# Dot products of the modulation on VectorE in both attention stages

## The chip, the cores and the metric

One core of a Trainium2 chip runs the whole program. The metric is the device time of one execution in microseconds; the time given is the median of three. The core has five engines that each work through their own queue in order: TensorE (PE; its weight loads are PEld), VectorE (DVE), ScalarE (ACT), GpSimd (POOL) and SyncE (SP), which here only issues transfers.

## The reference

The reference is three mixer layers over 512 tokens of width 2048, two of a first kind and one of a second. The first two also carry 256 context tokens. Each layer begins with a modulation: a vector `c` is passed through silu and multiplied with a matrix of 2048 x 6144, which gives a shift, a scale and a gate for every feature.

```python
sh_l, sc_l, g_l = jnp.split(jax.nn.silu(c) @ w_mod[l] + b_mod[l], 3, axis=-1)
sh_c, sc_c, g_c = jnp.split(jax.nn.silu(c_ctx) @ w_mod[l] + b_mod[l], 3, axis=-1)
hl = xl * (1.0 + sc_l[:, None, :]) + sh_l[:, None, :]
parts_l = jnp.split(hl @ w_in[l], SPLIT_POINTS, axis=-1)
```

The modulated tokens are multiplied with `w_in`; the parts feed a short convolution, a differential attention with eight heads, and a pooling branch. Their outputs are joined, multiplied with `w_out`, gated, added to the input and normalised. The third layer has its own modulation (`w_ada_2`) from `c_2`, a banded attention and a wider convolution.

## The kernel before, in words

All products with `w_in` and `w_out` are done on TensorE in a split of each fp32 number into a high part and the rest. A weight tile arrives in `wraw` (L155), ScalarE rounds it to `whi` (L156), GpSimd or VectorE subtracts to get `wlo` (L140), and TensorE multiplies high with high, high with rest and rest with high (`mm3`, L160 to L163). In the attention stages `wlo` is always GpSimd's (`lo_plan`). A `unit` (L195) is one such product of 128 features: 16 steps, into one or two of four PSUM buffers `ps_m`.

An attention stage (`attention`, L450) goes through eight heads. Each head has four units (query, key, value, gate). Their evictions follow: `evict_q` and `evict_k` turn the results by position (L314 to L317, on VectorE and GpSimd) and split them (L326 to L340), and `evict_v` copies the values out of PSUM on ScalarE (L345, L346) and transposes them. The tiles `qr` and `vT` of these three share one buffer, and each of the two key tiles has one buffer. So the value's copy waits until the key's split is done, and the key's split until the scores of the head before have been read out of the old key.

`attend` (L361) then works on blocks of 128 queries. For each of the two maps of a head: scores on TensorE (L379), a row maximum (L384) and its negative (L386) on VectorE, the exponential with its sum on ScalarE (L393), a reciprocal on VectorE (L395). L398, L400 and L401 on VectorE join both maps, TensorE transposes (L408), ScalarE and VectorE split (L412, L413), and TensorE multiplies with the values (L418). L422 to L446 are the norm of the head's output. The scores have one buffer (`ps_s`).

The modulation's products are spread as side work. Rows of the transposed matrix have 2048 numbers; a dot product of one such row per partition with silu(c) is done in four quarters of 512 (`dots`, L779). For every quarter the vector is loaded and passed through silu (L788 to L793), then each block of 128 rows is loaded as `gw` (L801; two buffers in the attention stages) and multiplied with one vector or two. The sum over the 512 goes to one column of the result; after each quarter but the first the columns are added (L815).

There are two ways of doing one such product. With `pool_every` at 0 it is one operation on VectorE, which multiplies and sums (L809). With `pool_every` at 1 it is a product on GpSimd into a junk tile with one buffer (L805), and a copy on ScalarE that sums it (L806). The two attention stages had 1; the stages between and after them have 0.

`along` hands such a generator to the main work, and `advance` takes a few steps of it (3 or 4) after every unit, with a priority that is 800 places later than the main work's. The order of every engine's queue is made when the program is built: a planner goes through all instructions by priority and by its own estimate of when each can start. So a change to some instructions can move others. What is left of the side work is issued by `finish` at the end of the stage.

The first stage has 192 such products (32 for the pooling's gates, 128 and 32 for the modulations of the first and the second layer), each load of `gw` being used for two vectors. The second has 128, each load for one.

Of the kernel before, what the change touches and what calls it, by code (L numbers as in the profile page):

```python
# [46 lines left out]
def mixer_stack_kernel(ctx: ExitStack, tc: tile.TileContext, a: dict, out: bass.AP):  # L47
# [8 lines left out]
    def pool(name, side):  # L56
        return tc.tile_pool(name=name, bufs=1, side=side, reuse_waits="tile")
# [113 lines left out]
    def along(steps, n):  # L171
        side["steps"], side["n"] = steps, n
# [6 lines left out]
    def finish():  # L179
        advance(10 ** 4)  # L180
        side["n"] = 0
# [268 lines left out]
    def attention(ap_, aq, l, w, H, Hc, started=None):  # L450
        cx = Hc if l == 0 else None
        T = NT if l == 0 else NL
        for h in range(8):
            if h == 0 and started:
                uq, uk, uv, ug = started
            else:
                uq = unit(w, 16 + h, H, cx)
            Q = evict_q(ap_, aq, uq, T)
            if not (h == 0 and started):
                uk = unit(w, 24 + h, H, Hc)  # L460
            K = evict_k(ap_, aq, uk)
            if not (h == 0 and started):
                uv = unit(w, 32 + h, H, Hc)
            vT = aq.tile([128, NT], F32, name="vT", tag="qr", bufs=1)
            V = evict_v(ap_, uv, vT)
            if not (h == 0 and started):
                ug = unit(w, 40 + h, H, cx)
            SG = ap_.tile([128, T], F32, name="SG", tag="SG", bufs=1)
            for ps, o, n in ((ug.lat, 0, NL), (ug.cx, NL, NCX)):
                if ps is not None:  # L470
                    th = aq.tile([128, NL], F32, name="rsh", tag="rsh", bufs=1)
                    silu2(SG[:, o:o + n], ps, th[:, :n])
            attend(ap_, l, h, Q, K, V, SG, T)
        for e in EARLY:
            if e[0] == l:
                u = unit(w, 48 + e[1], H, cx)
                t = aq.tile([128, NT], F32, name="pu", tag="qr", bufs=1)
                nc.scalar.copy(t[:, :NL], u.lat)
                if l == 0:
                    nc.scalar.copy(t[:, NL:], u.cx)  # L480
                nc.sync.dma_start(PUd[e][:, :T], t[:, :T])
# [209 lines left out]
    pgb = const.tile([128, 2, 4], F32, name="pgb")  # L691
# [87 lines left out]
    def dots(xp, vecs, scale, srcs, dst, bufs, pool_every=0):  # L779

        n = len(srcs)
        for q in range(4):
            sl = slice(q * 512, (q + 1) * 512)
            vs = []
            for v, src in enumerate(vecs):
                t = xp.tile([128, 512], F32, name=f"gv{v}", tag=f"gv{v}", bufs=1)
                if isinstance(src, str):
                    nc.sync.dma_start(t, Gd[src][0, sl].partition_broadcast(128))  # L788
                else:
                    nc.sync.dma_start(t, a["cc"][src, sl].partition_broadcast(128))  # L790
                    th = xp.tile([128, 512], F32, name="gw", tag="gw", bufs=bufs)
                    nc.scalar.activation(th, t, AF.Tanh, scale=0.5)
                    nc.vector.scalar_tensor_tensor(t, th, 1.0, t, op0=ALU.add, op1=ALU.mult)  # L793
                vs.append(t)
            part = dst
            if q:
                t = const.tile([128, 2, 32], F32, name="gpart", tag="gpart", bufs=1)
                part = [t[:, v] for v in range(len(vs))]
            for i, src in enumerate(srcs):
                w = xp.tile([128, 512], F32, name="gw", tag="gw", bufs=bufs)  # L800
                nc.sync.dma_start(w, src[:, sl])  # L801
                for v, t in enumerate(vs):
                    if pool_every and (i * len(vs) + v) % pool_every == 0:
                        pr = xp.tile([128, 512], F32, name="gpr", tag="gj", bufs=1)
                        nc.gpsimd.tensor_tensor(pr, w, t, op=ALU.mult)  # L805
                        nc.scalar.activation(pr, pr, AF.Copy, scale=scale, accum_out=part[v][:, i:i + 1])  # L806
                        continue
                    junk = xp.tile([128, 512], F32, name="gpr", tag="gj", bufs=1)
                    nc.vector.scalar_tensor_tensor(  # L809
                        junk, w, scale, t, op0=ALU.mult, op1=ALU.mult, accum_out=part[v][:, i:i + 1]  # L810
                    )
                yield
            if q:
                for d, p in zip(dst, part):
                    nc.vector.tensor_tensor(d[:, :n], d[:, :n], p[:, :n], op=ALU.add)  # L815

    def mod_dots(xp, names, vecs, w, bias, n0, n1, bufs=2, pool_every=0):
        dst = [mods[nm][:, n0:n1] for nm in names]
        yield from dots(xp, vecs, 0.5, [w[i] for i in range(n0, n1)], dst, bufs, pool_every)
        for d in dst:  # L820
            nc.vector.tensor_tensor(d, d, P(bias)[:, n0:n1], op=ALU.add)

    def mod_dots1(xp, l, n0, n1, bufs=2, pool_every=0):
        return mod_dots(xp, (f"l{l}", f"c{l}"), (0, 1), a["w_mod"][l], f"b_mod{l}", n0, n1, bufs, pool_every)

    def mod_dots2(xp, n0, n1, bufs=2, pool_every=0):
        return mod_dots(xp, ("s",), (2,), a["w_ada"][0], "b_ada", n0, n1, bufs, pool_every)

    with pool("attn0", R) as ap_:
        along(itertools.chain(  # L830
            dots(ap_, ("sh_l", "sh_c"), 1.0, [a["w_gateT"][g] for g in range(4)], [pgb[:, 0], pgb[:, 1]], 2, 1),
            mod_dots1(ap_, 0, 32, 48, 2, 1),
            mod_dots1(ap_, 1, 0, 4, 2, 1),
        ), 3)
        attention(ap_, ap_, 0, w0, H, Hc, started=us)
        finish()
# [62 lines left out]

    lo_plan["cycle"] = "P"  # L900
    with pool("attn1", L) as ap_:
        along(mod_dots2(ap_, 2, 34, 2, 1), 4)
        attention(ap_, aq, 1, a["w_in"][1], H, Hc)
        finish()
    es_q.close()
# [67 lines left out]
    with pool("attn2", R) as ap_:  # L973
# [25 lines left out]
        for j in range(2):  # L999
# [3 lines left out]
            for s in range(2):  # L1003
                g, r = 2 * j + s, 64 * s
# [5 lines left out]
        for j in range(2):  # L1010
# [7 lines left out]
            for s in range(2):  # L1018
                g = 2 * j + s
# [278 lines left out]
```

## Time and profile before

| | us |
|---|---|
| median of 3 runs | 3577.58 (3574.09 to 3579.79) |
| the profiled execution's own time | 3577.58 |
| its span, first to last instruction | 3575.8 |
| TensorE busy | 3301.2 |
| VectorE busy | 2324.2 |
| ScalarE busy | 1519.0 |
| GpSimd busy | 1958.8 |
| first attention stage, about | 245 to 1035 |
| second attention stage, about | 1630 to 2290 |

The profile names an engine, the line of the kernel and the tiles (output <- inputs) of every instruction. A busy time is a sum of instructions; an idle time stands before an instruction, with the releaser that ended it. The granted clock is TensorE's, as a share of full speed.

### The profile page before, as it was taken

How to read it: one execution, taken by the hardware profiler on the slowest of the kernel's cores; microseconds unless marked ns; L12 is line 12 of the kernel's file. 1: busy time of each engine (PE TensorE's matmuls, PEld its weight loads, DVE VectorE, ACT ScalarE, POOL GpSimd, SP SyncE). 2: the span in 40 equal slices, each digit the busy share in tenths (PEclk: the TensorE clock that was granted, in tenths of full speed). 3: DMA queues.
4: the chain of work that ended last, by engine and by line, in shares of the span. 5: the costliest groups of instructions: out<-in, count | busy, mean ns of one | idle time of the engine just before them, and what ended most of it. 6: DMA issues, size and time to landing. Idle time of an engine off the chain costs nothing.

```text
span 3575.8 us, 48562 instructions
## 1 busy us (share of the span) xinstructions
PE 3301.2 (92%) x16850; PEld 2791.3 (78%) x16850; DVE 2324.2 (65%) x3649; ACT 1519.0 (42%) x3181; POOL 1958.8 (55%) x1436
## 2 busy tenths in 40 slices
PE   8898998989998899999999999998989899999997
PEld 7787887878886787778888888877668777777765
DVE  6845555555468538774565555585577899996576
ACT  2255666655431222243665654322445333345333
POOL 2356776765234543256877764587776444444432
PEclk8899999989998999999999999999999999999999
DMA  8744333333246447664554542586765222223565
GB/s 311 288 133 115 99 111 99 103 104 89 70 143 185 135 131 221 191 223 140 159 154 143 162 126 85 184 309 227 231 221 195 80 93 84 84 77 109 183 222 187
DMA packets 274150, 554.72 MB, mean 155 GB/s; under 512 B 30992, under 2 KB 40048, under 8 KB 265712
## 3 DMA queue, kind: packets, MB, share of 16 engines
q1 hardware_dynamic: 271344, 539.04, 46.9%
q0 software_dynamic: 2560, 12.58, 1.8%
q8 instruction: 132, 2.16, 0.3%
q14 instruction: 114, 0.93, 0.1%
HBM read 510.69 MB, written 28.23 MB: 151 GB/s over the span
## 4 chain that ended last, share of the span: by engine, by line
PE 49%; DVE 18%; DMA 12%; issue 8%; POOL 7%; ACT 6%; SPq 0%; DVEq 0%; POOLq 0%; ACTq 0%
PE ps_m L163 35%; DVE acc L989 5%; DMA wraw<-in_w_out_dram 5%; POOL wlo L140 3%; POOL gpr L805 3%; DVE gpr L809 2%; PE ps_m L232 2%; PE ps_s L379 2%; ACT whi L156 2%; DVE wlo L140 2%; PE ps_v L418 2%; DMA gw<-in_w_ada_dram 1%; PE ps_s L233 1%; PE ps_m L609 1%; DMA gv<-in_cc_dram 1%
## 5 line engine op out<-in xcount | busy, mean ns | idle before, releaser
L163 PE MATMUL ps_m<-h,whi 128*128 128x512 f32 (+1 forms) x4736 | 1611.2, 398 | 47.3 <-ACT vT L345 32.5
L140 POOL TENSOR_TENSOR wlo<-wraw,whi 128x512 fp32r<-128x512 f32 x768 | 1113.3, 1467 | 947.6 <-ACT whi L156 886.0
L163 PEld LDWEIGHTS ps_m<-h,whi 128*128 128x128 f32 x4736 | 899.9, 192 | 233.7 <-ACT vT L345 34.1
L156 ACT CAST whi<-wraw 128x512 fp32r<-128x512 f32 x1040 | 608.1, 618 | 881.1 <-DMA wraw<-in_w_out_dram 268.0
L163 PE MATMUL ps_m<-h,wlo 128*128 128x512 f32 (+1 forms) x2368 | 940.0, 397 | 0.1
L805 POOL TENSOR_TENSOR gpr<-gw,gv 128x512 f32<-128x512 f32 x320 | 425.8, 1331 | 240.9 <-ACT gpr L806 173.1
L163 PE MATMUL ps_m<-hc,whi 128*128 128x256 f32 x2048 | 554.5, 283 | 0.0
L163 PEld LDWEIGHTS ps_m<-h,wlo 128*128 128x128 f32 x2368 | 455.1, 192 | 93.8 <-POOL wlo L140 0.8
L163 PEld LDWEIGHTS ps_m<-hc,whi 128*128 128x128 f32 x2048 | 381.0, 190 | 3.4
L140 DVE TENSOR_TENSOR wlo<-wraw,whi 128x512 fp32r<-128x512 f32 x272 | 246.7, 921 | 202.3 <-ACT whi L156 201.7
L806 ACT ACTIVATE gpr<-gpr 128x512 f32<-128x512 f32 x320 | 201.8, 631 | 233.6 <-POOL gpr L805 232.9
L163 PE MATMUL ps_m<-hc,wlo 128*128 128x256 f32 x1024 | 288.9, 282 | 0.0
L989 DVE SCALAR_TENSOR_TENSOR acc<-gu,pack,acc 128x511 f32<-128x511 f32 (+24 forms) x240 | 232.7, 981 | 5.4
L609 PE MATMUL ps_m<-wlo,y 128*128 128x512 f32 x512 | 208.1, 407 | 21.2 <-POOL wlo L140 13.6
L809 DVE SCALAR_TENSOR_TENSOR gpr<-gw,gv 128x512 f32<-128x512 f32 x232 | 220.7, 951 | 8.4 <-DMA gw<-in_w_ada_dram 2.0
L610 PE MATMUL ps_m<-whi,y 128*128 128x512 f32 x512 | 204.2, 400 | 3.2 <-DVE y L140 3.2
L384 DVE TENSOR_REDUCE mx<-ps_s 128x1 f32<-128x768 f32 (+1 forms) x160 | 135.0, 844 | 102.0 <-PE ps_s L379 101.2
L163 PEld LDWEIGHTS ps_m<-hc,wlo 128*128 128x128 f32 x1024 | 194.9, 190 | 1.0
L608 PE MATMUL ps_m<-whi,y 128*128 128x512 f32 x512 | 183.3, 400 | 1.7 <-ACT y L582 0.8
L413 DVE TENSOR_TENSOR aTl<-ps_t,aTh 128x384 fp32r<-128x384 f32 (+1 forms) x144 | 77.4, 538 | 156.2 <-ACT aTh L412 156.0
L609 PEld LDWEIGHTS ps_m<-wlo,y 128*128 128x128 f32 x512 | 98.0, 191 | 56.5 <-POOL wlo L140 22.1
L379 PE MATMUL ps_s<-K,Q 128*128 128x384 f32 x576 | 133.3, 347 | 9.5 <-ACT E L393 5.2
(353 smaller groups left out, 5284.4 us busy)
## 6 DMA issues: line engine op xcount, KB each, us to landing
wraw<-in_w_in_dram SPq DMA_DIRECT2D x640, 256.0 KB, 2.9
wraw<-in_w_out_dram SPq DMA_DIRECT2D x384, 256.0 KB, 3.5
wm<-in_w_mod_dram SPq DMA_DIRECT2D x48, 1024.0 KB, 6.9
gw<-in_w_mod_dram SPq DMA_DIRECT2D x192, 256.0 KB, 3.4
gw<-in_w_ada_dram SPq DMA_DIRECT2D x136, 256.0 KB, 3.2
wm<-in_w_ada_dram SPq DMA_DIRECT2D x14, 1024.0 KB, 6.5
K<-K POOLq DMA_DIRECT2D x32, 384.0 KB, 4.4
gv<-in_cc_dram SPq DMA_DIRECT2D x40, 256.0 KB, 3.6
```

The costliest lines, as they stand in the source:

```text
L140: eng.tensor_tensor(lo, src, hi.bitcast(F32), op=ALU.subtract)
L156: nc.scalar.copy(hi[:, sl], raw)
L163: nc.tensor.matmul(ps, w, mv[part], start=(first and p == 0), stop=(last and p == 2))
L379: nc.tensor.matmul(o, Qm[:, q0:q0 + 128], kp[:, c * ncol:(c + 1) * ncol], start=i == 0, stop=i == 1)
L384: nc.vector.reduce_max(mx, sv, axis=AX.XY)
L608: nc.tensor.matmul(ps, yh, hi[:, sl], start=(k == 0), stop=False)
L609: nc.tensor.matmul(ps, yh, lo[:, sl], start=False, stop=False)
L610: nc.tensor.matmul(ps, yl, hi[:, sl], start=False, stop=(k == KT - 1))
L805: nc.gpsimd.tensor_tensor(pr, w, t, op=ALU.mult)
L806: nc.scalar.activation(pr, pr, AF.Copy, scale=scale, accum_out=part[v][:, i:i + 1])
L809: nc.vector.scalar_tensor_tensor(junk, w, scale, t, op0=ALU.mult, op1=ALU.mult, accum_out=part[v][:, i:i + 1])
L989: nc.vector.scalar_tensor_tensor(A[:, s:], U[:, :NL - s], wj(i), A[:, s:], op0=ALU.mult, op1=ALU.add)
```

## The change

Five calls lose their last two arguments. `bufs` is 2 by default as well, so only `pool_every` changes, from 1 to 0. With 0, the branch with L805 and L806 is not taken, and every product of the two stages becomes L809. The transfers, the quarters and the additions of L815 stay the same in the source.

```diff
@@ -828,9 +828,9 @@
     with pool("attn0", R) as ap_:
         along(itertools.chain(
-            dots(ap_, ("sh_l", "sh_c"), 1.0, [a["w_gateT"][g] for g in range(4)], [pgb[:, 0], pgb[:, 1]], 2, 1),
-            mod_dots1(ap_, 0, 32, 48, 2, 1),
-            mod_dots1(ap_, 1, 0, 4, 2, 1),
+            dots(ap_, ("sh_l", "sh_c"), 1.0, [a["w_gateT"][g] for g in range(4)], [pgb[:, 0], pgb[:, 1]], 2),
+            mod_dots1(ap_, 0, 32, 48),
+            mod_dots1(ap_, 1, 0, 4),
         ), 3)
         attention(ap_, ap_, 0, w0, H, Hc, started=us)
         finish()
@@ -899,7 +899,7 @@
     with pool("attn1", L) as ap_:
-        along(mod_dots2(ap_, 2, 34, 2, 1), 4)
+        along(mod_dots2(ap_, 2, 34), 4)
         attention(ap_, aq, 1, a["w_in"][1], H, Hc)
         finish()
```

## Rows read from the trace of the kernel before

**Rows 1.** The page, part 1: busy us, share of the span, instructions.

```profile
PE 3301.2 (92%) x16850; PEld 2791.3 (78%) x16850; DVE 2324.2 (65%) x3649; ACT 1519.0 (42%) x3181; POOL 1958.8 (55%) x1436
```

**Rows 2.** Stretches: length, busy PE, PEld, DVE, ACT, POOL, granted clock, DMA share, GB/s.

```profile
245.00:890.00 645.00, 578.10 (x3361) 510.98 (x3361) 365.72 (x640) 389.46 (x911) 436.97 (x342) 0.94 0.36 104
890.00:1035.00 145.00, 138.45 (x812) 122.34 (x811) 62.57 (x132) 59.94 (x118) 37.78 (x30) 0.96 0.26 78
1630.00:2130.00 500.00, 487.22 (x2695) 424.89 (x2694) 286.99 (x447) 289.27 (x658) 381.15 (x300) 0.99 0.51 146
2130.00:2290.00 160.00, 160.00 (x832) 137.33 (x831) 73.54 (x130) 69.57 (x129) 62.04 (x51) 1.00 0.28 90
```

**Rows 3.** PE's waits, 245 to 1035: us in total, times, longest.

```profile
PE ps_m L163 <- ACT vT L345: 32.5, 5, 8.9
PE ps_t L408 <- DVE E L401: 12.0, 3, 5.8
```

**Rows 4.** PE's waits, 1630 to 2290.

```profile
PE ps_t L408 <- DVE E L401: 7.2, 3, 4.2
```

**Rows 5.** Timeline of PE: start us, us, instruction, idle before it and its releaser.

```profile
434.39 0.69 PE L408 MATMUL ps_t<-ident,E 128*128 128x128 f32 x2 [5.82 <-DVE E L401]
```

**Rows 6.** Timeline of VectorE in the same stall.

```profile
427.60 4.32 DVE L400 TENSOR_SCALAR E<-E,rd 128x256 f32<-128x256 f32 x1
```

**Rows 7.** Timeline of GpSimd in the same stall.

```profile
427.45 0.57 POOL L341 DMA_DIRECT2D K<-K  x1 [1.22 <-DVE K L140]
428.04 1.29 POOL L805 TENSOR_TENSOR gpr<-gw,gv 128x512 f32<-128x512 f32 x1
429.28 2.48 POOL L140 TENSOR_TENSOR wlo<-wraw,whi 128x512 fp32r<-128x512 f32 x2
```

**Rows 8.** Groups, 890 to 1035: busy us, mean ns, idle before.

```profile
L400 DVE TENSOR_SCALAR E<-E,rd 128x256 f32<-128x256 f32 x4 | 1.6, 404 | 0.1
```

**Rows 9.** Timeline of VectorE in the second stage.

```profile
1901.00 7.14 DVE L398 TENSOR_TENSOR rd<-rd,neglam 128x1 f32<-128x1 f32 x1
```

**Rows 10.** The stretch of that operation, columns as in rows 2.

```profile
1901.00:1908.20 7.20, 4.17 (x19) 3.08 (x17) 7.16 (x2) 2.73 (x7) 7.12 (x6) 1.00 0.99 237
```

**Rows 11.** Groups, 2130 to 2290, columns as in rows 8.

```profile
L398 DVE TENSOR_TENSOR rd<-rd,neglam 128x1 f32<-128x1 f32 x8 | 1.3, 159 | 0.2
```

**Rows 12.** The stretch after the stall of rows 5, columns as in rows 2.

```profile
430.60:440.60 10.00, 6.21 (x16) 4.92 (x17) 8.39 (x12) 5.61 (x14) 5.32 (x5) 0.50 0.47 119
```

**Rows 13.** Tile gpr alone: busy DVE, ACT, POOL in two stretches, clock, DMA.

```profile
245.00:890.00 645.00, 0.00 (x0) 138.62 (x384) 252.66 (x192) 0.94 0.36 104
1630.00:2130.00 500.00, 0.00 (x0) 92.40 (x256) 173.14 (x128) 0.99 0.51 146
```

**Rows 14.** ScalarE's waits, 245 to 1035, columns as in rows 3.

```profile
ACT gpr L806 <- POOL gpr L805: 132.9, 105, 4.0
```

**Rows 15.** The page, part 5: busy us, mean ns, idle before, releaser.

```profile
L809 DVE SCALAR_TENSOR_TENSOR gpr<-gw,gv 128x512 f32<-128x512 f32 x232 | 220.7, 951 | 8.4 <-DMA gw<-in_w_ada_dram 2.0
```

**Rows 16.** Line L809: duration ns minimum, median, maximum, first and last start.

```profile
L809 DVE SCALAR_TENSOR_TENSOR gpr<-gw,gv x232: 670/693/2194, 1038.2 to 1515.1; 128x512 f32<-128x512 f32 x116
L809 DVE DVE_READ_ACCUMULATOR gpr<-gw,gv x232: 74/81/88, 1039.8 to 1516.6; 128x1 f32 x116
```

**Rows 17.** Groups, 245 to 890, columns as in rows 8.

```profile
L400 DVE TENSOR_SCALAR E<-E,rd 128x256 f32<-128x256 f32 x12 | 17.7, 1472 | 0.4
L398 DVE TENSOR_TENSOR rd<-rd,neglam 128x1 f32<-128x1 f32 x40 | 16.9, 422 | 1.3
```

**Rows 18.** Groups, 1630 to 2130, columns as in rows 8.

```profile
L398 DVE TENSOR_TENSOR rd<-rd,neglam 128x1 f32<-128x1 f32 x24 | 21.7, 906 | 0.8
```

**Rows 19.** GpSimd's waits, 1630 to 2290, columns as in rows 3.

```profile
POOL gpr L805 <- DMA gw<-in_w_ada_dram: 25.7, 18, 3.3
```

**Rows 20.** SP's queue's waits, 245 to 890, columns as in rows 3.

```profile
SPq L801 <- POOL gpr L805: 226.1, 74, 7.8
```

## The prediction

> **What bounds the kernel now.** I read the busy times first, then the stretches, then the waits, then single timelines. TensorE is busy 92% of the span and is the engine to watch [rows 1]. The change touches only the two attention stages, at 245 to 1035 us and 1630 to 2290 us. I cut each where its last product on GpSimd ends, at 890 and at 2130 us. In the first stage TensorE is idle 645 - 578.1 = 66.9 us (10.4%) while the dot products run, at a granted clock of 0.94, and 6.6 of 145 us (4.5%) at 0.96 after them. In the second it is idle 12.8 of 500 us (2.6%) at 0.99 with them, and not at all at 1.00 after them [rows 2]. So the first stage has something to win, and the second very little.
>
> What TensorE waits for in the first stage is led by ScalarE's copy of V out of PSUM (L345, 32.5 us in 5 waits) and VectorE's last softmax step (L401, 12.0 us in 3) [rows 3]. In the second L401 gives 7.2 us in 3 [rows 4]. These fall where one head ends and the next is prepared. One is shown: TensorE stands 5.82 us until 434.39 for L401 [rows 5]. Behind that lies L400 on VectorE, which took 4.32 us from 427.60, although the same form takes 0.404 us after the dot products. From 427.45 to 431.76 GpSimd ran a DMA issue, a product (gpr) and two subtractions (wlo), almost without a gap, and L400 ended 0.16 us after the last of them [rows 6 to 8]. L398 in the second stage took 7.14 us from 1901.00, with GpSimd busy in six operations for 7.12 us of the same stretch, where 0.159 us is its mean after the dot products [rows 9 to 11]. A stall costs twice: in the 10 us from 430.6 the granted clock is 0.50, which is 1.2 of 2.4 GHz [rows 12].
>
> **The change part by part.** Removed from GpSimd: 320 products, 252.7 us in the first stage and 173.1 us in the second. Removed from ScalarE: 320 sums with their accumulator reads, 138.6 and 92.4 us [rows 13], and the time in which its queue stood for a product, 132.9 us in the first stage [rows 14]. On ScalarE those waits stood ahead of the exponentials, the K copies and the V copy. The junk tile that passed from GpSimd to ScalarE and back now stays on one engine, so two waits per dot product go and none is added to it.
>
> Added to VectorE: 320 operations of the form of L809. Its floor is 0.693 us (the median) and its mean 0.951 us, with 0.08 us for the accumulator read [rows 15, 16]. I take 0.951 + 0.08 = 1.03 us, because GpSimd still runs wlo beside it: 192 x 1.03 = 198 us and 128 x 1.03 = 132 us. Given back: L398 falls to its mean after the dots, (422 - 159) ns x 40 = 10.5 us and (906 - 159) ns x 24 = 17.9 us, and the narrow form of L400 gives (1472 - 404) ns x 12 = 12.8 us [rows 8, 11, 17, 18]. VectorE then has 365.7 - 23.3 + 198 = 540 of 645 us (84%) and 287.0 - 17.9 + 132 = 401 of 500 us (80%), from 57% each [rows 2]. It fits, so VectorE doesn't become the bound by its sum. It can by its order.
>
> Term 1, the first stage's stalls. If the dot products cost TensorE nothing, the stretch would look like the one after them: (10.4 - 4.5)% of 645 = 38 us, and 0.02 of clock over 645 us = 13 us, 51 us together. Below, the least is nothing at all, if the stalls come from the order of the evictions alone. I take two thirds, 34 us, since in the stall shown (4.32 - 0.40) of 5.82 us was the wait behind GpSimd.
>
> Term 2, the second stage: 12.8 us of idle and 0.01 of clock over 500 us, 18 us at most, nothing at least. Two thirds is 12 us.
>
> Term 3, what the new operations cost at the ends of heads. In the 10 us after the stall shown VectorE was busy 8.39 us, so 1.6 us were free [rows 12]. Spread evenly, 192 operations over 645 us put three into such a stretch. One fits, two delay the K subtraction that stands behind them, and with it ScalarE's V copy and TensorE: 2 x 1.03 = 2.1 us for each of seven ends (eight heads share 790 us, so 645 us hold six to seven), 14 us, and 4 us for the half clock behind longer stalls: 18 us. The bounds are 0 us (all fall where VectorE waits anyway) and 3 x 2.19 us (the longest L809) x 7 = 46 us. Between heads I cost them at nothing: TensorE has the next head's projections to do, and in that cover the softmax may come late. Without it 198 us would show.
>
> Term 4, the DMA. In the second stage GpSimd stood 25.7 us in 18 waits for the row of w_ada to land [rows 19]. That wait is now VectorE's, and behind it in the queue stand the row maxima, reciprocals and subtractions, which ScalarE's exponentials and TensorE's transposes wait for. TensorE's work hides most: 4 us, a sixth, between 0 and 25.7. No DMA is added or moved in the source. SP's queue stood 226.1 us in the first stage for products to release the two gw buffers, with the weight loads behind it [rows 20]; VectorE releases them now, after one operation rather than after a product that itself waited for ScalarE. I count nothing for it.
>
> Sum: -34 - 12 + 18 + 4 = -24 us. The profiled execution took 3577.58 us for a span of 3575.8 us, and it is itself the median of the three runs, so no other correction: 3577.6 - 24 = 3553.6 us, forecast 3554.
>
> That GpSimd holds VectorE off is first of all the row of 7.14 us. The Trainium skill's page "SBUF — State Buffer" (Who interferes with whom) states why: a VectorE operation with two SBUF inputs shares a read port with a GpSimd operation that reads SBUF, and the second to issue is blocked until the first finishes. On which operations meet, the trace agrees. On the length it doesn't: L398 stood through six GpSimd operations, not one [rows 10]. By the rule only one GpSimd operation of a stall would be won back, and the fourth rival below gives the sum for that.
>
> **The rivals.** The planner orders every queue anew at build time, by costs that the trace doesn't show, so each case carries some 10 us of unknown order (an estimate from the size of one or two stalls like the 5.82 us one).
>
> Slower, by VectorE's order at the ends of heads: GpSimd's pair of wlo runs just there (429.28 in the stall shown), so new operations are held up to 2.19 us each, ahead of the K subtraction. Three per end, each halfway between the mean and the longest, are 3 x 1.61 x 7 = 34 us, and 11 us more at half clock. Of terms 1 and 2 a third is left (23 us): 34 + 11 - 23 + 4 = +26 us, 3603 us. It decides from two new operations per end on: one fits into the 1.6 us. For it: VectorE has 84% to do. Against: ScalarE is freed of 139 us of sums and 133 us of standing, and V's copy, which TensorE waits for most, is ScalarE's.
>
> No change: the new operations meet wlo as L398 met gpr. The port waits that they bring, 320 x (951 - 693) ns = 83 us, exceed the 41 us that L398 and L400 lose. Then stalls only change their owner: 3578 us, within 7.
>
> All of it: every new operation falls into VectorE's idle time: -51 - 18 = -69 us, 3509 us. For it: while the dots run in the second stage TensorE is at 97% already, so there the softmax has slack. Against: 890 to 1035 us has no next head to prepare.
>
> Little is won per stall: VectorE waits out one GpSimd operation, and the rest of a stall has other causes. Then one product of 1.29 us goes of 5.82, 22%: -11 - 4 + 18 + 4 = +7 us, 3585 us. The row of 7.14 us speaks against it.
>
> **How the numbers follow.** The forecast has 50%, all of it 10%, no change 13%, the slower order 20%, one operation's length 7%. Within 0.2% is 7 us here, about what can be told from no change. Faster: 60%; same: 13%; slower: 27%. The range goes from 3512 (just inside the full gain) to 3603 us (the slower rival). The forecast's own range is 3535 to 3570.
>
> **What would show it.** Right: L805 and L806 are gone and L809 has 552 instructions at 0.9 to 1.0 us; L398 and L400 come down to 0.16 to 0.3 us and, in the narrow form, to under 0.9 us; TensorE's idle time in the first stage falls by 20 us or more; its waits for L345 halve; no VectorE operation takes over 4 us. Wrong: TensorE's idle time in the first stage grows, with waits for L345 or L401 behind an L809; VectorE waits over 10 us for gw; or TensorE's idle time stays and only its releasers have other names. The second stage losing more than 10 us of TensorE's time would refute term 4.

## The result: slower by 4%, and the profile after

The changed kernel takes 3728.8 us (median of 4 runs, 3724.0 to 3736.1), the kernel before 3578.7 us beside it: a ratio of 1.0419, 95% interval 1.0403 to 1.0436. The forecast was 3554 us, the range ended at 3603. Not only the size is off, but also the sign.

Busy times after, as in [rows 1]:

```profile
PE 3342.6 (90%) x16850; PEld 2809.4 (75%) x16850; DVE 2497.6 (67%) x4289; ACT 1315.4 (35%) x2541; POOL 1561.0 (42%) x1116
```

The work moved as it should: ScalarE and GpSimd each do some 200 to 400 us less, VectorE does 173 us more. Over the whole span VectorE still looks free, at 67%. The stretches tell otherwise. These are the two attention stages after the change, each cut where its last dot product ends (columns as in [rows 2]):

```profile
245.00:600.00 355.00, 271.89 (x1442) 231.15 (x1443) 283.65 (x664) 114.63 (x228) 93.46 (x66) 0.88 0.46 130
600.00:1095.00 495.00, 461.37 (x2701) 407.64 (x2701) 247.09 (x485) 209.61 (x416) 139.19 (x114) 0.96 0.22 64
1700.00:2080.00 380.00, 310.24 (x1564) 261.49 (x1563) 245.66 (x511) 114.78 (x226) 134.15 (x104) 0.91 0.52 150
2080.00:2380.00 300.00, 297.73 (x1658) 260.88 (x1657) 154.42 (x284) 138.42 (x261) 115.94 (x95) 1.00 0.25 78
```

The dot products now end at 600 us, where they ended near 890 before. In the stretch that holds them TensorE is idle for 83.1 of 355 us, and its granted clock is 0.88. The sum over both parts of the first stage, 83.1 + 33.6 = 116.7 us idle, stands against 73.5 before [rows 2], 43 us more. The clock lost 0.12 x 355 + 0.04 x 495 = 62 us, against 44.5 before, 18 us more. Together that is 61 us, and the first copy of the next stage (L499) indeed starts 61.8 us later, at 1085.5 in place of 1023.7. In the second stage idle time and clock come to 106 us against 18, 88 us more; its successor is 87 us later still, at 2368.9 in place of 2219.9. So the whole loss lies in the two stages, and each us of added idle time came with 0.4 to 0.5 us more at the lower clock.

TensorE's longest waits in the first stage, from 240 to 1050 us, to be set beside [rows 3], and in the second, from 1690 to 2400 us, beside [rows 4]:

```profile
PE ps_m L163 <- ACT vT L345: 35.3, 7, 6.5
PE ps_t L408 <- DVE E L401: 30.4, 10, 6.0
PE ps_s L379 <- ACT E L393: 11.8, 10, 4.8
```

```profile
PE ps_t L408 <- DVE E L401: 25.3, 5, 6.6
PE ps_t L408 <- DVE aTl L413: 17.2, 7, 5.1
```

The wait for ScalarE's copy of V (L345) did not halve; it rose by 2.8 us. The waits for VectorE's last softmax step (L401) went from 12.0 to 30.4 us and from 7.2 to 25.3 us; those for the exponential (L393) and for L413 were 5.2 and 2.0 us before. L809 itself, on the page, and then line L809 from 245 to 600 and from 1740 to 2080 us (minimum, median and maximum in ns, first and last start):

```profile
L809 DVE SCALAR_TENSOR_TENSOR gpr<-gw,gv 128x512 f32<-128x512 f32 x552 | 493.6, 894 | 154.1 <-DMA gw<-in_w_ada_dram 95.5
```

```profile
L809 DVE SCALAR_TENSOR_TENSOR gpr<-gw,gv x191: 628/692/1797, 247.2 to 593.7; 128x512 f32<-128x512 f32 x191
L809 DVE SCALAR_TENSOR_TENSOR gpr<-gw,gv x128: 629/693/4617, 1748.4 to 2067.0; 128x512 f32<-128x512 f32 x128
```

The duration is close to the forecast, 0.894 us against 0.951. The place is not: 191 of the 192 operations lie in 347 us, not 645, and 128 in 319 us, not 500. The idle time of VectorE before L809 by stage, in its groups from 245 to 600 us and from 1740 to 2080 us:

```profile
L809 DVE SCALAR_TENSOR_TENSOR gpr<-gw,gv 128x512 f32<-128x512 f32 x191 | 157.1, 822 | 48.0 <-DMA gw<-in_w_mod_dram 37.5 <-DMA gv<-gd_sh_c 4.1 <-DMA gw<-in_w_gateT_dram 2.5
```

```profile
L809 DVE SCALAR_TENSOR_TENSOR gpr<-gw,gv 128x512 f32<-128x512 f32 x128 | 113.0, 883 | 94.7 <-DMA gw<-in_w_ada_dram 94.0
```

An engine that waits at the head of its queue is as closed to the others as a busy one. Busy or standing before an L809, VectorE is taken for 283.7 + 48.0 = 331.7 of 355 us (93%) and for 245.7 + 94.7 = 340.4 of 380 us (90%). While the dot products last, VectorE is the suspect. That it is the bound does not follow from this share alone: a version further down has the same 90% in its second stage and hardly loses.

One stall shows how that reaches TensorE. This is the timeline of the changed kernel from 1950 us (start, duration, engine, line, operation, tiles; in brackets the idle time before and its releaser):

```profile
1950.35 6.87 SPq L801 DMA_DIRECT2D gw<-in_w_ada_dram  x3
...
1953.03 0.19 ACT L393 ACTIVATION_READ_ACCUMULATOR ps_s<-ps_s,nb 128x1 f32 x1
...
1955.82 1.03 DVE L809 SCALAR_TENSOR_TENSOR gpr<-gw,gv 128x512 f32<-128x512 f32 x1 [3.08 <-DMA gw<-in_w_ada_dram]
...
1956.78 0.15 DVE L395 RECIPROCAL rd<-dn 128x1 f32<-128x1 f32 x1
1956.97 1.02 DVE L398 TENSOR_TENSOR rd<-rd,neglam 128x1 f32<-128x1 f32 x1
1957.31 0.38 SPq L155 DMA_DIRECT2D wraw<-in_w_in_dram  x1
1958.02 1.02 DVE L401 SCALAR_TENSOR_TENSOR E<-ps_s,rd,E 128x768 f32<-128x768 f32 x1
...
1959.19 0.87 PE L408 MATMUL ps_t<-ident,E 128*128 128x128 f32 x3 [6.52 <-DVE E L401]
```

ScalarE has the sum of the exponential at 1953.22. The reciprocal that needs it (L395) starts at 1956.78, because an L809 ahead of it in VectorE's queue stands 3.08 us for its DMA and then runs 1.03 us. TensorE is idle for 6.52 us in the end. The Trainium skill's page "PSUM — Partial Sum Buffer" (Engine vs sequencer instructions) says that the queues of ScalarE, VectorE and GpSimd are strict FIFO; the 3.56 us between ready and started here agree with it. SP's queue has its own such place: three loads of gw, each after its buffer, take 6.87 us, and the next load of a weight tile follows only at 1957.31. SP's waits from 1690 to 2100 us after the change ([rows 20] is the same view for the first stage of the kernel before):

```profile
SPq L801 <- DVE gpr L809: 89.4, 86, 4.7
SPq L801 <- DMA gw<-in_w_ada_dram: 87.1, 79, 3.8
SPq L155 <- POOL wlo L140: 70.9, 28, 19.0
```

In the same 410 us of the kernel before, L801 stood 175.4 us for GpSimd's products and 19.4 us for landings. So the sum of SP's waits for gw did not grow; only single places, as the one shown, are worse.

### The profile page after: what moved, and what is told of

Read it like the earlier page. It is cut to its first block, busy times and chain, and to the rows that moved or that the text cites. A ratio compares the mean times of both kernels' runs of the same rounds, so it can differ in the third digit from the quotient of the medians.

```text
span 3722.2 us, 48214 instructions
## 1 busy us (share of the span) xinstructions
PE 3342.6 (90%) x16850; PEld 2809.4 (75%) x16850; DVE 2497.6 (67%) x4289; ACT 1315.4 (35%) x2541; POOL 1561.0 (42%) x1116
## 4 chain that ended last, share of the span: by engine, by line
PE 40%; DVE 24%; DMA 20%; issue 8%; ACT 4%; POOL 3%; SPq 1%; DVEq 0%; ACTq 0%; POOLq 0%
PE ps_m L163 29%; DVE gpr L809 8%; DMA gw<-in_w_ada_dram 5%; DVE acc L989 5%; DMA wraw<-in_w_out_dram 4%; DMA gw<-in_w_mod_dram 3%; DVE wlo L140 2%; POOL wlo L140 2%; DMA gv<-in_cc_dram 2%; PE ps_s L379 2%; ACT whi L156 2%; PE ps_v L418 1%; PE ps_m L232 1%; DMA wm<-in_w_ada_dram 1%; DMA wraw<-in_w_in_dram 1%
## 5 line engine op out<-in xcount | busy, mean ns | idle before, releaser
L140 POOL TENSOR_TENSOR wlo<-wraw,whi 128x512 fp32r<-128x512 f32 x768 | 1131.4, 1490 | 1570.7 <-ACT whi L156 1484.1
L809 DVE SCALAR_TENSOR_TENSOR gpr<-gw,gv 128x512 f32<-128x512 f32 x552 | 493.6, 894 | 154.1 <-DMA gw<-in_w_ada_dram 95.5
L384 DVE TENSOR_REDUCE mx<-ps_s 128x1 f32<-128x768 f32 (+1 forms) x160 | 135.3, 846 | 104.6 <-PE ps_s L379 103.5
L413 DVE TENSOR_TENSOR aTl<-ps_t,aTh 128x384 fp32r<-128x384 f32 (+1 forms) x144 | 77.4, 538 | 124.5 <-ACT aTh L412 124.3
L379 PE MATMUL ps_s<-K,Q 128*128 128x384 f32 x576 | 143.3, 364 | 18.9 <-ACT E L393 13.8
L408 PE MATMUL ps_t<-ident,E 128*128 128x128 f32 x416 | 76.2, 290 | 87.0 <-DVE E L401 55.7
L412 ACT CAST aTh<-ps_t 128x384 fp32r<-128x384 f32 (+1 forms) x144 | 67.2, 467 | 241.5 <-PE ps_t L408 241.3
L282 DVE SCALAR_TENSOR_TENSOR wm<-wm,ca 128x2048 f32<-128x2048 f32 x50 | 124.7, 2494 | 23.6 <-DMA wm<-in_w_ada_dram 15.3
```

The costliest lines, as they stand in the source:

```text
L140: eng.tensor_tensor(lo, src, hi.bitcast(F32), op=ALU.subtract)
L282: nc.vector.scalar_tensor_tensor(pr, wm, scale, ca, op0=ALU.mult, op1=ALU.mult, accum_out=dst)
L379: nc.tensor.matmul(o, Qm[:, q0:q0 + 128], kp[:, c * ncol:(c + 1) * ncol], start=i == 0, stop=i == 1)
L384: nc.vector.reduce_max(mx, sv, axis=AX.XY)
L413: nc.vector.tensor_tensor(dl, tv, dh.bitcast(F32), op=ALU.subtract)
L809: nc.vector.scalar_tensor_tensor(junk, w, scale, t, op0=ALU.mult, op1=ALU.mult, accum_out=part[v][:, i:i + 1])
```

## The experiments

Each median stands beside runs of the kernel before on the same chip; I compare ratios. "The first copies" are the first starts of L499 behind each attention stage (1023.7 and 2219.9 us before; 1085.5 and 2368.9 us after); they mark the ends of the two stages. In the diffs, `held` is on only in the two attention stages.

**One stage alone.** The second stage goes back to GpSimd and ScalarE.

```
-        along(mod_dots2(ap_, 2, 34), 4)
+        along(mod_dots2(ap_, 2, 34, 2, 1), 4)
```

> Only the first attention stage has its dot products on VectorE; the second has them on GpSimd and ScalarE as before. In the changed kernel the first convolution unit came 62 us later than before and everything after the second stage 149 us later, so 62 us belong to the first stage and 87 us to the second. Theory A (the planner packs the new operations, one between nearly every two steps of the softmax, and each stands in that chain) and theory B (they stand at the head of VectorE's queue until their row gw has landed, 38 us in the first stage and 94 us in the second) both expect the parts to add: 3578 + 62 = 3640 us, within 10. If the stages don't add (a common cause such as a shift of the weights' loads), it comes out under 3610 or over 3670.

3660.8 us, 1.0217 (1.0197 to 1.0238), some 16 us above the sum that both theories expected. The first copy of the first stage is 69 us late (1092.7), where it was 62 us late in the changed kernel, and the second (2301.0) adds 12. So the first stage by itself costs 78 us, and 72 us of the 150 are left for the second. That the two simply add is not shown, since the second stage alone was not run.

**No wait for gw.** The loads stay, the dot products read a table that lies in SBUF.

```
                 w = xp.tile([128, 512], F32, name="gw", ...)
                 nc.sync.dma_start(w, src[:, sl])
+                if held["on"]:
+                    w = rope_c
```

> All loads of gw stay, but the dot products of both attention stages read a tile that is there from the start, so that none waits for a load (this leaves out the right result of those products). Theory B: the 134 us of waits go, and with them nearly all of the loss: 3580 to 3620 us. Theory A: the operations are as many and are packed at least as tightly, so the softmax is as late: 3690 to 3760 us, and VectorE's idle time before L809 is near nothing.

3711.1 us, 1.0358 (1.0337 to 1.0378). At first sight the waits are then worth some 20 us. That reading does not hold: loads that nothing reads are no longer paced, and ScalarE's silu step (L792), whose tile takes its turn in the same two buffers, then stood up to 17.8 us for them. The run without loads, below, takes its place.

**Three buffers for gw in the second stage.**

```
-                    junk = xp.tile([128, 512], F32, name="gpr", tag="gj", bufs=1)
+                    junk = w if bufs == 3 else xp.tile(...)
...
-        along(mod_dots2(ap_, 2, 34), 4)
+        along(mod_dots2(ap_, 2, 34, 3), 4)
```

> In the second stage alone gw has three buffers in place of two (the junk is written over the row, which makes the room). Theory B: half or more of the 94 us of waits goes, and 40 to 60 us of time: 3670 to 3690 us. Theory A: the loads come earlier, the planner packs the operations tighter, and the time stays within 20 us of 3729.

3724.2 us, 1.0394 (1.0373 to 1.0415). VectorE's waits for the row of w_ada fell from 94.0 to 55.4 us, and nothing that is clear of the noise was won by it:

```profile
DVE gw L809 <- DMA gw<-in_w_ada_dram: 55.4, 53, 2.6
```

With the earlier loads the planner packed the operations closer: they run from 1750 to 1996 us, where they ran from 1748 to 2067.

**Spread by a marker.** The factor of each product is read from a small tile that VectorE writes when a unit is done, so that no dot product can come before its unit. (The 32 products for the gates are not marked, and the junk tile is in bfloat16.)

```
     unit_steps(w, n, operands(*parts))
+    if mark:
+        side["at"] = const.tile([128, 1], F32, name="mark", ...)
+        nc.vector.tensor_scalar(side["at"], u.lat[:, :1], 0.0, 0.5, op0=ALU.mult, op1=ALU.add)
...
-    junk, w, scale, t, ...
+    junk, w, side["at"], t, ...
```

> The factor 0.5 of the dot products is read from a number that VectorE writes when a query, key or gate unit is done, so that the operations of the modulation can't start before the unit at which the source puts them: some 20 for every 10 row maxima all through both stages, in place of 63, 65, 48 and 16 in the first 40 row maxima (the 32 for the gates stay unpaced; the junk tile is bf16, for room). Same operations, same loads, same two gw buffers. Theory A: most of the loss goes, 3560 to 3620 us. Theory B: three or four operations still come together with two buffers, so a third to a half of the waits stays: 3630 to 3680 us, with 50 us or more of waits for gw on VectorE.

3672.6 us, 1.0255 (1.0238 to 1.0272). Some 59 us of the 150 are won, 91 stay, which is the second expectation. The waits in the second stage show a cost that the marker itself brought: each unit's end now releases operations of VectorE just ahead of the gate's eviction (L245, L241 in the other kernels), and TensorE waited for that 26.8 us in six:

```profile
PE ps_m L163 <- DVE SG L245: 26.8, 6, 5.2
```

**Neither loads nor dot products, and each alone.** Without dot products the sums are set to zero; without loads the products read the table.

```
-                for v, t in enumerate(vs):
+                for v, t in enumerate(vs if not held["on"] else ()):
```

> Loads and modulation vectors stay, the dot products of both attention stages are left out (their sums are set to zero, so the output is not the reference's). This gives the floor. Theory A (the dot products on GpSimd and ScalarE cost TensorE little before, the stalls of the kernel before come from the softmax chain itself): 3545 to 3580, within 30 of the time before, so the change had little to win and the whole rise of 150 is what VectorE's operations cost. Theory B (the prediction's first two terms: the stalls of before come from GpSimd's dot products): 3500 to 3535.

> Neither the loads of gw nor the dot products in the two attention stages (their sums are set to zero; output not the reference's). The floor of the stages. Theory L (the kernel without dot products at 3671 was slow because its loads, which nothing paces, come between the loads of the next head's weights): 3555 to 3590. Theory O (something else in the changed order costs the 90 us there, with no load and no dot product needed for it): 3640 to 3680.

> All dot products on VectorE as after the change, but of a table in SBUF; the loads of gw are left out (output not the reference's). Theory Q (the operations in VectorE's queue, packed, are what costs): 3670 to 3720. Theory L (the loads bunched together with the weights' loads are what costs; then the kernel with loads kept and dot products of a table, 3711, was slow by its loads): 3580 to 3625.

Neither: 3551.5 us, 0.9917 (0.9902 to 0.9932), 3.5 us under the range of theory L. Dot products on VectorE without loads: 3654.1 us, 1.0202 (1.0186 to 1.0217). Loads without dot products: 3671.6 us, 1.0256 (1.0240 to 1.0271), outside both expectations. The kernel without loads lies between its two theories, nearer to the queue's. The one with neither is the floor: loads and dot products together cost the kernel before some 30 us, 0.8%, and that is about what any placement of them could win.

The stretch of the second stage in which the dot products without loads lie, 1718 to 1912 us, shows VectorE busy for 183.2 of 194 us (94%) and TensorE for 160.2; without any side work TensorE is busy for 389.2 of 390 us:

```profile
1718.00:1912.00 194.00, 160.24 (x802) 135.03 (x801) 183.22 (x381) 60.12 (x117) 70.58 (x51) 0.91 0.23 66
```

```profile
1690.00:2080.00 390.00, 389.20 (x2206) 343.06 (x2206) 196.74 (x368) 174.60 (x331) 154.57 (x125) 1.00 0.26 76
```

So VectorE's operations alone, packed, cost (1.0202 - 0.9917) x 3580 = 102 us, with no load of gw in it. The loads alone cost 121 us, but in a way of their own. In that kernel from 1809 us seven loads of gw went out in one row on SP, ScalarE's silu step stood for its buffer among them, and TensorE was idle for 21.27 us:

```profile
1809.04 10.05 SPq L801 DMA_DIRECT2D gw<-in_w_ada_dram  x7
...
1819.19 0.38 SPq L155 DMA_DIRECT2D wraw<-in_w_in_dram  x1
...
1831.33 0.63 ACT L792 ACTIVATE gw<-gv 128x512 f32<-128x512 f32 x1 [19.66 <-DMA gw<-in_w_ada_dram]
...
1833.42 0.58 PE L418 MATMUL ps_v<-aTh,Vh 128*128 128x256 f32 x1 [21.27 <-ACT aTh L412]
```

In the changed kernel VectorE's reading paces the loads and ScalarE's step waits only for its own vector, so these 121 us are not a term of the change. They show what happened with loads that nothing paced.

**The marker again, without waits for gw.**

> The paced kernel with the dot products reading a table that is already in SBUF, the loads kept (output not the reference's): no operation of VectorE waits for gw. Theory A (what is left of the rise once the operations are spread, 89 us, is the operations' own 1 us in the queue of the softmax steps): 3650 to 3675. Theory B (it is the wait for gw at the head of VectorE's queue, 68 us of waits in the paced profile): 3600 to 3630.

> The same without loads of gw, and the dot products spread by the marker as in the paced kernel (output not the reference's). Theory Q: the operations' own microsecond in the queue remains, 3620 to 3660. Theory L: 3570 to 3600.

With unpaced loads 3697.1 us, 1.0328 (1.0301 to 1.0355), outside both expectations: that run has the fault of unpaced loads once more. Three stalls of 23 us in its second stage end with L245, which waits for the output transfer of the head before, and SP issues that behind seven loads of gw each time (10.28 to 11.15 us). Without loads 3651.3 us, 1.0199 (1.0182 to 1.0216), as much as packed. That looks like a cost of the operation itself, wherever it stands; the next runs speak against it. In the second stage the cost is mostly the marker's: TensorE is idle for 33.3 of 580 us there, 26.6 of them in six waits for L245. Why the first stage ends 24 us late (first copy at 1047.5) is open.

**An engine that paces.** Four versions in which a second engine takes a part: ScalarE the sums, GpSimd and ScalarE every second dot product, GpSimd the products, GpSimd a copy of gw.

> Product on VectorE, sum on ScalarE in place, one product buffer: VectorE has an operation for each dot product as after the change, but a second engine paces them (38 per ten row maxima in place of 65). Theory A (density of the operations among the softmax steps): between the paced kernel and the one after, 3640 to 3700. Theory B (only the fused operation is dear, or the loss is the missing pace): 3570 to 3610. Theory C (any VectorE operation there costs its whole time, whatever the density): 3715 to 3750, as ScalarE gets its sums back.

```
-                        nc.gpsimd.tensor_tensor(pr, w, t, op=ALU.mult)
+                        nc.vector.tensor_tensor(pr, w, t, op=ALU.mult)
                         nc.scalar.activation(pr, pr, AF.Copy, scale=scale, accum_out=...)
```

> Every second dot product stays on GpSimd and ScalarE as before, the others on VectorE; products in bfloat16. Theory A (the cost goes by how many VectorE operations stand per softmax step, 26 per ten row maxima): 3600 to 3640. Theory C (each VectorE operation costs the same share, 145 / 2): 3640 to 3665. Rival: both engines in the chain is worse than either: above 3665.

> Product on GpSimd as before, sum on VectorE (one operation of 128x512 per dot product): VectorE still has an operation for each, but GpSimd waits for gw, frees its buffer and paces both loads and sums (about 25 per ten row maxima). Theory Q (each operation in VectorE's queue costs by itself): 3630 to 3670, as the paced kernel. Theory L (loads in bursts, and VectorE's wait for them, are the cost): 3580 to 3610.

```
                         nc.gpsimd.tensor_tensor(pr, w, t, op=ALU.mult)
-                        nc.scalar.activation(pr, pr, AF.Copy, scale=scale, accum_out=...)
+                        nc.vector.tensor_reduce(part[v][:, i:i + 1], pr, axis=AX.X, op=ALU.add)
```

> VectorE has the change's own fused operation for every dot product, but on a copy of the weight tile that GpSimd makes first (one buffer), so that GpSimd waits for gw and sets the pace: 19 to 23 operations per ten row maxima where the changed kernel has 65. Theory pace (packing and bursts of loads are the cost): 3585 to 3620. Theory op (a fused operation of 1 us in VectorE's queue costs its 0.2 us wherever it stands): 3645 to 3680.

```
-                        nc.gpsimd.tensor_tensor(pr, w, t, op=ALU.mult)
-                        nc.scalar.activation(pr, pr, AF.Copy, scale=scale, accum_out=...)
+                        nc.gpsimd.tensor_copy(pr, w)
+                        nc.vector.scalar_tensor_tensor(pr, pr, scale, t, op0=ALU.mult, op1=ALU.mult, accum_out=...)
```

Product on VectorE, sum on ScalarE: 3692.4 us, 1.0317 (1.0301 to 1.0334), as density has it, though VectorE still stands for its loads there (74.4 us for the row of w_ada). Every second dot product on VectorE: 3751.3 us, 1.0479 (1.0464 to 1.0495), slower than all others, against theories A and C; the rival, that both engines in the chain are worse than either, has it right. Product on GpSimd, sum on VectorE: 3598.3 us, 1.0046 (1.0030 to 1.0062), not the 3630 or more of the theory that every operation costs by itself. GpSimd's copy, then the change's own operation on VectorE: 3592.7 us, 1.0057 (1.0036 to 1.0078).

The last one decides between the operations themselves and their pace. VectorE has all 320 operations of the change, at the change's length, and the time is 0.6% over the kernel before, not 4.2%. What differs from the changed kernel is that GpSimd reads gw first. The operations then lie over the whole stage:

```profile
L806 DVE SCALAR_TENSOR_TENSOR gpr<-gpr,gv x190: 627/684/3196, 244.6 to 995.5; 128x512 f32<-128x512 f32 x190
L806 DVE SCALAR_TENSOR_TENSOR gpr<-gpr,gv x128: 628/683/1784, 1691.3 to 2225.1; 128x512 f32<-128x512 f32 x128
```

And in the stretches of the first and the second stage TensorE is idle for 38.4 of 355 us and for 15.0 of 390 (36.9 and 11.1 in the kernel before):

```profile
245.00:600.00 355.00, 316.62 (x1848) 280.79 (x1847) 255.55 (x526) 143.95 (x285) 170.32 (x176) 0.94 0.34 97
...
1690.00:2080.00 390.00, 375.05 (x2069) 327.87 (x2067) 272.99 (x527) 161.39 (x311) 216.58 (x216) 0.98 0.49 140
```

In this second stage VectorE is busy for 273 us of 390, not less than in the changed kernel's 246 of 380. So it is not how much VectorE does. What is left is how close the operations stand and what they stand waiting for. This is the count of dot products in VectorE's queue, as the programs were built, between each ten row maxima (L384) of the softmax; a stage has 96 or 64 of these:

```
                                first stage                          second stage
changed kernel                  63 65 48 16  0  0  0  0  0  .   | 49 51  5  0  0  0
VectorE's, without loads        69 63 57  3  0  0  0  0  0  .   | 78 15  0  0  0  0
VectorE product, ScalarE's sum  40 38 37 38 33  6  0  0  0  .   | 43 44 22  0  0  0
every second on VectorE         27 25 25 19  0  0  0  0  0  .   | 23 25  7  0  0  0
GpSimd's product, VectorE's sum 26 27 21 25 24 24 25 20  0  .   | 26 29 29 25 10  0
GpSimd's copy first             22 20 20 20 19 19 22 19 18  .   | 23 23 21 21 20 12
marker, without loads           32 10 17 19 18 24 18 24 30  .   | 24 16 24 16 24  4
```

(The ten maxima that straddle the two stages are left out.) With every second one on VectorE the other half stands on GpSimd and ScalarE in the same stretch, to 635 us, so some 50 dot products per ten maxima stand there too, on three engines; why that is slowest of all is not shown.

The count does not settle the time alone. The marker's kernel without loads spreads its operations about as far as GpSimd's copy does and loses 2%, for the reason given in the second stage and an open one in the first. Nor does the share of VectorE's time settle it. With GpSimd's product and VectorE's sum, VectorE in the second stage is busy for 274.9 of 380 us and stands 67.9 us before its sums, 90% together, as after the change; TensorE is idle there for 18.9 us, not for 69.8:

```profile
1700.00:2080.00 380.00, 361.12 (x1975) 312.85 (x1974) 274.88 (x439) 152.86 (x296) 288.74 (x225) 0.98 0.57 152
```

```profile
L806 DVE TENSOR_REDUCE gpart<-gpr 128x1 f32<-128x512 f32 x80 | 54.4, 680 | 40.8 <-POOL gpr L805 40.4
L806 DVE TENSOR_REDUCE mod_s<-gpr 128x1 f32<-128x512 f32 x31 | 21.1, 682 | 27.1 <-POOL gpr L805 26.9
```

What the two fast versions share is that GpSimd, and not VectorE, reads gw, and that 29 operations at most stand between ten maxima.

**The loads at that pace.** The copy on GpSimd, no dot product (sums set to zero).

> The loads and GpSimd's copies of them, no dot product (sums set to zero, output not the reference's). Theory burst (loads cost only where runs of them stand ahead of the next head's weights in SP's queue): 3550 to 3575, by the floor of 3551. Theory bandwidth (67 MB of loads through the attention stages cost as such): 3620 to 3670, by the 3671 of the unpaced loads.

3535.5 us, 0.9902 (0.9885 to 0.9919), below both expectations, and the floor again within the noise. GpSimd's copies end at 820 and 2093 us there, earlier than with the dot products behind them (1004 and 2223). In the second stage TensorE has no idle time at all at 156 GB/s, which is more than the 150 of the changed kernel's:

```profile
1690.00:2080.00 390.00, 390.00 (x2207) 343.52 (x2206) 218.58 (x370) 175.67 (x336) 229.24 (x239) 1.00 0.53 156
```

So the loads, read by GpSimd, cost nothing that shows. From here the price of one dot product follows: (1.0057 - 0.9902) x 3580 = 55 us for 320 that are spread on VectorE, 0.17 us each; 35 us for those of the kernel before, 0.11 us each. Packed on VectorE without loads it was 102 us over the floor, 0.32 us each.

**Is there a faster version?** The products of the kernel before, denser, less dense, or with the sums on two engines; and the copy in the first stage alone.

> All products on GpSimd (in bfloat16), the sums in turn on VectorE and ScalarE, each with a product buffer of its own. If pace decides: 3570 to 3605, denser than before with 35 dot products per ten row maxima, VectorE's half 18. If two engines in the chain cost more than one, above 3610.

> The kernel before with two product buffers in bfloat16 in place of one: GpSimd does not wait for ScalarE's sum. If the loads' bursts cost once GpSimd runs ahead: 3585 to 3620, if GpSimd's wait for ScalarE was what cost: 3555 to 3572.

```
-  pr = xp.tile([128, 512], F32, name="gpr", tag="gj", bufs=1)
+  pr = xp.tile([128, 512], BF16, name="gpr", tag="gj", bufs=2)
```

> The kernel before with one gw buffer in place of two: no load of gw can be sent while the last one is still read, so the order on GpSimd is less dense (34 products per 32 weight tiles in the second stage, where the kernel before has 45). Theory pace: 3555 to 3572, faster than before. Rival: GpSimd waits for each load at the head of its own queue (some 3 us from issue to landing, 224 loads), the low parts of the weights stand behind it, and the next head's units come late: 3590 to 3650.

> First attention stage as in the kernel with GpSimd's copy and VectorE's fused operation, second as before. If the stages add up as their traces say: 10 us under the kernel before, 3562 to 3574. If the 10 us are the planner's chance, or lost again in other stages: 3575 to 3600.

Sums in turn on VectorE and ScalarE: 3641.7 us, 1.0195 (1.0175 to 1.0216), 37 us above what pace had it at, and on the side of the other theory, that two engines in the chain cost more than one. Two product buffers: 3613.1 us, 1.0119 (1.0102 to 1.0137); GpSimd's products then end at 709 us in the first stage and 2065 in the second, not at 864 and 2110. VectorE does not take part in that, and TensorE's waits for L401 in the first stage are 25.5 us in 8 all the same, against 12.0. So pace is not a matter of VectorE alone. One gw buffer: 1.0373 (1.0359 to 1.0387). The theory of pace fails there. The sign is the rival's, but the 134 us are nearly twice the most that I gave it (72), and that GpSimd's wait for each load is the cause is not shown. The copy in the first stage alone: 3587.3 us, 1.0017 (1.0008 to 1.0026). The 10 us that I expected to win did not come: the first copy started at 1023.2 us, where it had started at 1017.9 with GpSimd's copy in both stages. Of the kernels that do the whole work none beats the one before.

## Why the prediction was wrong

*What bounds the kernel.* Half right. TensorE was idle in the first stage and could win little in the second. But I put the first stage's idle time down to the dot products because it fell from 10.4 to 4.5% after them. The run without any side work is the check: 29 us less for both stages, of which the first copy shows 11 us in the first stage (1012.3 against 1023.7). There the wait for L345 is 38.6 us in 7, no less than with the dot products.

*Terms 1 and 2, -46 us.* Too large: the floor allows 29 us, and the rival with all of it (3509) was out of reach. L398 did come down, from 422 to 288 ns and from 906 to 451 ns, but TensorE's waits did not go with it. The wait behind GpSimd in the one stall that I had followed was real. That another cause stood ready behind it fits the floor's 38.6 us for L345, but was not followed stall by stall.

*Term 3, +18 us, is the step that failed.* "Spread evenly, 192 operations over 645 us put three into such a stretch", and "between heads I cost them at nothing". I took over the density of the kernel before. As I read the runs, that density was the work of what the change removed: one junk buffer that passed from GpSimd to ScalarE and back, so each dot product waited for the last. (Two such buffers on GpSimd already cost 43 us.) On VectorE a dot product waits for nothing but its load, and the planner packed them: 63 and 65 stand between ten row maxima in the first stage, six to each softmax step, some 5 us of VectorE per step. In place of 18 us the packed operations cost 102 us over the floor, with no load of gw at all. My sum of 84 and 80% over 645 and 500 us became 93 and 90% over 355 and 380 us, waits included. In the cover between heads "the softmax may come late", I wrote, "without it 198 us would show": in the half of the stage that held them TensorE's work did not cover it, and it was idle for 83.1 of 355 us. The rival that I gave for the slower side (3603) saw VectorE's order, but only at the heads' ends and at the old density.

*Term 4, +4 us, bounds 0 to 25.7.* Mis-sized. VectorE stood 94.0 us in 77 waits for the row of w_ada, where GpSimd had stood 25.7 in 18. The bound was a row of the old pace. The two waits per dot product that I counted as gone had, as I read it, also kept the loads ahead of their readers. By the sign that I set myself, more than 10 us lost in the second stage (59 us of added idle time), the term is refuted; how many us the waits alone cost is not settled.

How the 150 us divide: against the kernel before, packing on VectorE without loads is 1.0202 (72 us) and the rest, up to 1.0419, is 78 us with the loads. VectorE's waits for gw and the weight loads kept back on SP, as in the stall shown, are the candidates; how much goes to which is not settled. Three buffers cut the waits and raised the density, so they told nothing of it, and the runs with unpaced loads brought a fault of their own. With GpSimd reading gw, packing and waits go together, so those runs do not part them either. Why the planner packs just so also stays open, since its own estimates show in no trace.

*The port rule.* After the change the longest L398 took 1.226 us, where one took 7.14 before [rows 9], and one of GpSimd's wlo takes 1.490 us on average. But an L809 took 4.62 us, against its median of 0.693, while GpSimd ran four such subtractions without a gap, the first begun 0.9 us before it and the last ended 0.6 us before its end:

```profile
1757.21 4.62 DVE L809 SCALAR_TENSOR_TENSOR gpr<-gw,gv 128x512 f32<-128x512 f32 x1 [1.73 <-DMA gw<-in_w_ada_dram]
```

```profile
1756.31 4.96 POOL L140 TENSOR_TENSOR wlo<-wraw,whi 128x512 fp32r<-128x512 f32 x4
```

So the sign "no VectorE operation takes over 4 us" failed too: the long holds did not go with GpSimd's products. The Trainium skill's page "SBUF — State Buffer" (Summary: rules for kernel authors) has the second operation wait until the first is finished. On the length the new trace does not agree with that any more than the old one.

## What to carry to other kernels

Before side work is moved to an engine that seems free, find what spaced it: a single buffer between two engines, or a slower engine that takes the wait for the DMA, can be the pace that keeps it out of the critical chain, and it goes with the "overhead". Count the moved operations per step of the critical chain in the new order, and add the waits at the head of the new queue to its busy time; a share of the whole span hides both. Neither number gives the loss by itself: one version here had the same share and hardly lost, another had the spread and lost 2%. And run the kernel without the side work first: here that floor was some 1% away, and no placement could win much more.

## What the runs showed of the hardware

- Idle time of TensorE came with more on top: 43 us more idle with 18 us at the lower clock in the first stage, 59 with 29 in the second. The granted clock of the stretches with stalls was 0.88 and 0.91, a mean of its two levels; without stalls it was 1.00.
- A copy of 128x512 on GpSimd took 0.615 us (median), the product of the same shape 1.292 us. 320 such copies, which also took the waits for the loads, cost nothing that could be seen (0.9902 against the floor's 0.9917).
- 156 GB/s of DMA traffic stood beside a TensorE without idle time, so bandwidth was not what these stages lacked.
- One operation of VectorE can be held through several of GpSimd: 4.62 us through four subtractions after the change, where the median is 0.693 us.
